# One core, fp32 trunk layer: the gate stage's second half regrouped, its weights' lower parts moved to the vector engine, and the norms' roots taken by a GpSimd power

## The chip, the core and the metric

The kernel runs on one NeuronCore of a Trainium2 chip. The core has a matrix engine (PE), a vector engine (DVE), an activation engine (ACT), GpSimd (POOL) and a sync engine (SP) that issues transfers here. Each works through its own queue in order, and they wait for one another by semaphores. Matmul results land in PSUM banks, from which DVE or ACT fetch them; GpSimd does not touch PSUM in this kernel. The metric is device time in microseconds for one launch. Before the change it is 930.51 us, the median of three runs (929.92 to 930.7).

## The reference

One layer over 1024 tokens and 1024 features, fp32: an input projection feeds a pooling mixer and a gated linear recurrence, an output projection returns to the residual stream `h`, a squared-ReLU MLP follows, and then the part that the change touches most:

```python
def rms_norm(x, g):
    y = x * lax.rsqrt(jnp.mean(x * x, axis=-1, keepdims=True) + RMS_EPS)
    return y * g
...
    z = rms_norm(h, norm_mlp_g[l])
    h = h + jnp.square(jax.nn.relu(z @ w_up[l])) @ w_down[l]
    z = rms_norm(h, norm_ple_g[l])
    gate = jax.nn.sigmoid(z @ w_ple_gate[l] + b_ple_gate[l])
    h = h + gate * (p[l] @ w_ple_proj[l])
return rms_norm(h, norm_final_g)
```

There are four norms: before the input projection, before the MLP, before the gate, and at the end. `w_ple_gate` is 1024x1024, `p` has 256 features.

## The kernel before, in words

Everything is held transposed: features on the 128 partitions, tokens along the free dimension, so `h` is eight tiles `H[0..7]` of 128 features by 1024 tokens. A product of two fp32 matrices is made of three matmuls of a reduced-precision fp32 type: each operand is split into an upper part (an ACT cast, line 176, or 179 with a gain) and a lower part (DVE's difference to it, line 177 or 180), and `mm` (line 340) issues upper·upper, upper·lower and lower·upper, 128 x 128 weights against up to 512 tokens each.

The MLP runs as a fast matrix scheme with seven products per block (`up_pair`, `down`), whose sums DVE builds. The code is a program for a scheduler: it places every instruction on its engine's queue by dependencies and priorities, and `keep_in_program_order` (`pin`), `issue_after` and `high_priority` bind it in places. Buffers come from pools with a fixed number of slots; PSUM offers two double banks (`banks`) and four single ones (`bank`).

A norm (class `Norm`, line 373) squares each tile on ACT, adds the squares on DVE, splits the sum and multiplies it with a matrix of ones on PE, so that each partition holds the sum over all features. `rstd` (line 427) then transposes blocks of 32 on DVE, so that one column in 32 holds all different values, takes square root with scale 1/D and bias eps on ACT (line 436) and the reciprocal on DVE (line 437) of these few columns (`edge`, 16 for 512 tokens, 8 for 256), and transposes them back into `R` (line 438). ACT's functions come in tables; going from one set to another costs a table load on ACT.

The gate stage (lines 1078 to 1136) goes through groups of tokens: 0 to 511, 512 to 767, 768 to 1023. In each group it goes through the eight output tiles in the order `ORDER[g]`. Per output PE does six matmuls for `p @ w_ple_proj` and 24 for the gate (`ple_proj`, `ple_gate`), each as wide as the group. `ple_out` multiplies the gate's bank by `R` on DVE (line 1034), applies the sigmoid on ACT (1035), multiplies with the projection (1040), adds to `h` (1041) and adds the square for the last norm (387, 388). For the last group the operand is normalised beforehand (`ple_in_normed`, 907), so that its sigmoid reads PSUM directly (1032). The weights of outputs 0 to 3 pass through two slots and are fetched again (`FETCH`) for the second and third group, with the lower part on POOL; those of 4 to 7 stay in `B`. When all outputs of a group are done, `finish` (1052) takes the final norm's root and scales each tile of the group by `g_fin` and the root (1058), spread over later outputs by `DONE` and `LAST`, and stores. The last group ends in `finish_last` (1065): gains are applied before the root is known, and four products (1075) and stores follow it.

At the start ten warm-up matmuls on ones run while the first tiles of x arrive (457), and a small activation makes `eps` (371).

Of the kernel before, what the change touches and what calls it, by code (L numbers as in the profile page):

```python
# [12 lines left out]
P = 128  # L13
S = 1024
# [10 lines left out]
AHEAD = ((0,), (1, 2), (3,), ())  # L25
IN = {("P5", 2): (0, 1), ("P5", 3): (2, 3), ("P3", 0): (4, 5), ("P3", 1): (6, 7)}
LATER = ((), (0, 1), (2, 3), (4, 5), (6, 7), (), ())
GROUPS = (slice(0, 512), slice(512, 768), slice(768, 1024))
NT = D // P

ORDER = ((0, 1, 2, 3, 4, 5, 6, 7), (2, 3, 4, 5, 6, 7, 0, 1), (0, 1, 4, 5, 6, 7, 2, 3))

DONE = (((), (), (0,), (1,), (2,), (3,), (4,), (5,)), ((6,), (7,), (), (), (), (), (), ()))
LAST = ((), (), (0, 1), (2, 3), (4, 5), (6, 7), (), ())
FETCH = ((0, 1, 2, 3), (0, 1), (2, 3))
NLRU = 4
NPOOL = 4
WINDOWS = (2, 4, 8, 16)
# [18 lines left out]
def block_kernel(  # L57
# [264 lines left out]
    todo += [(up_step, m, step) for m in range(NPAIR) for step in range(4)]  # L322
    todo += [(down_step, c, kind, q) for c, kind in KINDS for q in range(NQ)]
    for g, os in enumerate(FETCH):
        todo += [
            (load_weights, w_gate[o], f"wg{g}_{o}", S, nc.gpsimd if g else None) for o in os
        ]
    todo.reverse()
    asked = []

# [36 lines left out]
    ones = pool.tile([P, P], F32R, name="ones")  # L367
    nc.vector.tensor_copy(ones, T[4][:, :P])
    ones_f = f32(ones)
    eps = pool.tile([P, 1], F32, name="eps")  # L370
    nc.scalar.activation(eps, ones_f[:, :1], AF.Copy, scale=EPS)

    class Norm:

# [29 lines left out]
        def sums(self, halves=HALVES, cast=False):  # L404

            parts = []
            for hs in halves:
                hi, lo = self.parts(hs)
                o = bank(f"{self.name}_ps{hs.start}")[:, : hs.stop - hs.start]
                in_order[:] = [True] * cast  # L410
                if not cast:
                    nc.vector.tensor_copy(hi, self.acc[:, hs])
                    nc.vector.tensor_tensor(lo, self.acc[:, hs], f32(hi), ALU.subtract)
                pin(nc.tensor.matmul(o, ones, hi, start=True, stop=False))
                pin(nc.tensor.matmul(o, ones, lo, start=False, stop=True))
                in_order.clear()
                parts.append((hs, o))
            return parts

        def sums_of(self, hs, squares):  # L420

            o = bank(f"{self.name}_ps{hs.start}")[:, : hs.stop - hs.start]
            for n, sq in enumerate(squares):
                nc.tensor.matmul(o, ones_f, sq, start=n == 0, stop=n == len(squares) - 1)
            return [(hs, o)]

        def rstd(self, out, parts=None):


            for hs, o in parts or self.sums():  # L430
                r = out[:, hs]
                nc.vector.transpose(r, o)
# [3 lines left out]
                nc.scalar.activation(few, r[:, :, 0], AF.Sqrt, bias=eps, scale=1.0 / D)  # L436
                nc.vector.reciprocal(few, few)
                nc.vector.transpose(r, few.unsqueeze(2).broadcast_to([P, n, 32]))

    def tables():  # L440

        one = ones_f[:, :16]
# [9 lines left out]

    norm = Norm("n0", T[0], T[1:3])
    ps_l = [psum(f"ps_l{o}") for o in range(3)]
    wide = ones.unsqueeze(1).broadcast_to([P, HALF // P, P])
    for _ in range(WARM):
        nc.tensor.matmul(ps_l[2][0][1][:, :HALF], ones, wide, start=True, stop=True)
# [138 lines left out]
    def pool_windows(g, ps):  # L596
        w = WINDOWS[g]
        u, *st = T[:3]
        if ps:
            normed(u, ps)  # L600
        cur = st[g % 2]
        if w == 2:
            nc.vector.tensor_tensor(cur[:, 1:], u[:, 1:], u[:, : S - 1], ALU.add)
            nc.vector.tensor_copy(cur[:, :1], u[:, :1])
        else:

            nc.vector.tensor_tensor_scan(cur[:, :w], ones_f[:, :w], u[:, :w], 0.0, ALU.mult, ALU.add)
# [290 lines left out]
        n = (k % 2) * HALF + hs.start % HALF  # L898
        return [x[:, n : n + hs.stop - hs.start] for x in pair]

    def ple_in(o, hs, norm, to=None):

        to = to or hs
        split(H[o][:, to], *z3(o, to), col("g_ple", o))
# [97 lines left out]
    root = pool.tile([P, 1], F32, name="root")  # L1002

    def ple_psum(g, hs, o, apart):
        turn.append(o)
# [59 lines left out]
    def finish_last(hs, end, squares):  # L1065
# [7 lines left out]
        for o in [*(o for o in range(0, NT, 2) if o != low), low]:  # L1073
            os = slice(o, o + 2)
            nc.vector.tensor_tensor(done[:, os], h_all[:, os, hs], r, ALU.mult)
            nc.sync.dma_start(out_end[:, os], done[:, os])

    for g, hs in enumerate(GROUPS):
        for n, o in enumerate(ORDER[g]):
            pg, pj = ple_psum(g, hs, o, hs == GROUPS[-1] and n == NT - 1)  # L1080
            if g == 0 and n < 2:
                ple_gate(g, hs, o, pg, n == 1)
                held.append((o, pg, pj))
# [7 lines left out]
            elif g == len(GROUPS) - 1 and n == NT - 1:  # L1091
                ple_gate(g, hs, o, pg)
                ple_proj(hs, o, pj)
            else:
                ple_proj(hs, o, pj)
                ple_gate(g, hs, o, pg)
# [3 lines left out]
                split(raw, *B[n + 3])  # L1100
                gate_p[n + 3] = B[n + 3]

            end = g == len(GROUPS) - 1
            if (g > 0 or n > 1) and not (end and n == NT - 1):
                ple_out(hs, o, pg, pj, not end or n < 6)
            if g == 0 and n > 0:
                for o in LATER[n - 1]:
                    ple_in(o, SECOND, norm2, GROUPS[1])
# [4 lines left out]
            if end and n < 6:  # L1113
                gain(o, hs)
            if end and n == NT - 1:
# [11 lines left out]
                in_order.clear()  # L1127
                nc.vector.tensor_tensor(sqs[1], H[o][:, hs], H[o][:, hs], ALU.mult)
                squares += sqs
            if g > 0:  # L1130
                finish(GROUPS[0], DONE[g - 1][n])
# [78 lines left out]
```

## Time and profile before

| | us |
|---|---|
| median of three runs | 930.51 |
| span of the profiled execution, first to last instruction | 929.2 |
| PE busy | 916.9 |
| DVE busy | 766.3 |
| ACT busy | 456.7 |
| POOL busy | 14.9 |

The profiled execution is one of its own; its span does not hold the little that lies before the first and after the last instruction, and 930.51 − 929.2 = 1.3 us stand for that.

In the profile, a group's row names line, engine, operation, output<-inputs (tile names without their numbers), shape and count. A row of the timeline begins with the start and the duration in microseconds; a bracket at its end tells how long the engine was idle before and what released it. "The chain" is the sequence of work that ended last, followed back from the end; its rows are start, duration, engine, tile and line. A row of stretches gives the stretch, its length, and the busy time of PE, weight loads, DVE, ACT and POOL with the number of instructions, then the granted TensorE clock and the transfers' share. Matmuls are pipelined: the duration of one is longer than the distance to the next.

### The profile page before, as it was taken

The numbers are of one execution on the slowest core, as the hardware profiler recorded it, in microseconds if no ns is written. First come the engines' busy times: TensorE is split into PE (matmuls) and PEld (weight loads), VectorE is DVE, ScalarE is ACT, GpSimd is POOL, SyncE is SP. The second block draws the span as 40 slices with busy tenths as digits, with TensorE's granted clock in tenths as the row PEclk, the third lists the DMA queues.
The fourth block names the chain that finished last, engine by engine and source line by source line (L and its number), as shares of the span: only waits on it lengthen the run. The fifth ranks groups of instructions, "written<-read, shape, count | busy, mean of one in ns | idle before, by whom it ended". The sixth has DMA issues, their size and how long they took to land.

```text
span 929.2 us, 11479 instructions
## 1 busy us (share of the span) xinstructions
PE 916.9 (99%) x4472; PEld 804.3 (87%) x4472; DVE 766.3 (82%) x926; ACT 456.7 (49%) x544; POOL 14.9 (2%) x11
## 2 busy tenths in 40 slices
PE   9999999999999999999999999999999999999996
PEld 7888888888888888888888888888888888888995
DVE  7997984669998888888888989979776679885976
ACT  7467892447543443343334545434343446653445
POOL 0000000002000000000000000000000000000220
PEclk9999999999999999999999999999999999999999
DMA  7310143212154355345434998366522441031122
GB/s 259 104 47 25 44 161 111 68 45 75 64 189 161 126 179 194 125 147 187 165 125 157 362 352 272 120 206 209 190 92 91 136 136 45 23 119 41 46 92 91
DMA packets 45189, 125.03 MB, mean 135 GB/s; under 512 B 4176, under 2 KB 6224, under 8 KB 45136
## 3 DMA queue, kind: packets, MB, share of 16 engines
q1 hardware_dynamic: 44992, 124.27, 39.3%
q8 instruction: 35, 0.57, 0.3%
q14 instruction: 18, 0.15, 0.0%
q10 hardware_dynamic: 144, 0.04, 0.0%
HBM read 90.74 MB, written 33.55 MB: 134 GB/s over the span
## 4 chain that ended last, share of the span: by engine, by line
PE 91%; DVE 5%; ACT 2%; DMA 1%; issue 1%; SPq 0%; DVEq 0%; ACTq 0%
PE ps_P_u L350 31%; PE ps_P_d L350 30%; PE ps_i L350 10%; PE ps_o L350 9%; PE ps_e L350 6%; PE ps_l L350 3%; DVE h L1041 1%; PE ps_j L350 1%; DMA wd<-act 1%; PE ps_g L553 1%; DVE a L177 1%; DVE h L1058 1%; DMA h<-in_xT 1%; PE ps_p L350 1%; DVE t L1040 0%
## 5 line engine op out<-in xcount | busy, mean ns | idle before, releaser
L350 PE MATMUL ps_P_d<-a,wd_P_hi 128*128 128x512 f32 x880 | 261.7, 379 | 0.0
L350 PEld LDWEIGHTS ps_P_d<-a,wd_P_hi 128*128 128x128 f32 x880 | 166.3, 189 | 23.6
L350 PE MATMUL ps_P_d<-a,wd_P_lo 128*128 128x512 f32 x440 | 166.9, 379 | 0.7 <-DVE wd_P_lo L177 0.7
L350 PE MATMUL ps_P_u<-a,wu_hi 128*128 128x512 f32 x512 | 152.3, 379 | 0.0
L350 PE MATMUL ps_P_u<-y,wu_hi 128*128 128x512 f32 x384 | 114.0, 379 | 0.0
L350 PEld LDWEIGHTS ps_P_u<-a,wu_hi 128*128 128x128 f32 x512 | 96.8, 189 | 13.8
L350 PE MATMUL ps_P_u<-a,wu_lo 128*128 128x512 f32 x256 | 97.0, 379 | 0.0
L350 PEld LDWEIGHTS ps_P_d<-a,wd_P_lo 128*128 128x128 f32 x440 | 83.2, 189 | 12.9 <-DVE wd_P_lo L177 1.1
L350 PEld LDWEIGHTS ps_P_u<-y,wu_hi 128*128 128x128 f32 x384 | 72.6, 189 | 10.3
L729 DVE TENSOR_TENSOR t<-t,ps_P_u 128x512 f32<-128x512 f32 (+1 forms) x80 | 62.5, 781 | 20.3 <-PE ps_P_u L350 20.2
L350 PE MATMUL ps_i<-a,wi_hi 128*128 128x512 f32 x288 | 74.3, 380 | 0.0
L350 PE MATMUL ps_P_u<-y,wu_lo 128*128 128x512 f32 x192 | 72.8, 380 | 0.0
L177 DVE TENSOR_TENSOR a<-wd,a 128x1024 fp32r<-128x1024 f32 x56 | 67.3, 1218 | 2.4 <-ACT a L176 2.0
L176 ACT ACTIVATE a<-wd 128x1024 fp32r<-128x1024 f32 x56 | 58.8, 1053 | 20.3 <-DMA wd<-act 11.9
L350 PE MATMUL ps_o<-y,wo_hi 128*128 128x512 f32 x256 | 65.7, 379 | 0.0
L350 PEld LDWEIGHTS ps_i<-a,wi_hi 128*128 128x128 f32 x288 | 54.1, 189 | 8.8 <-issue 1.0
L176 ACT ACTIVATE wu_hi<-wu 128x1024 fp32r<-128x1024 f32 x24 | 25.4, 1057 | 69.8 <-PE ps_P_u L350 48.5
L176 ACT ACTIVATE wu_hi<-wu_raw 128x1024 fp32r<-128x1024 f32 (+1 forms) x25 | 25.1, 1006 | 66.9 <-PE ps_P_u L350 41.5
L350 PEld LDWEIGHTS ps_o<-y,wo_hi 128*128 128x128 f32 x256 | 48.4, 189 | 6.8
L350 PEld LDWEIGHTS ps_P_u<-a,wu_lo 128*128 128x128 f32 x256 | 48.4, 189 | 6.8
L176 ACT ACTIVATE wd_P_hi<-wd 128x1024 fp32r<-128x1024 f32 x24 | 25.3, 1054 | 48.9 <-PE ps_P_d L350 44.7
L387 ACT ACTIVATE t<-h 128x512 f32<-128x512 f32 (+2 forms) x47 | 32.8, 697 | 28.0 <-DVE h L1041 19.8
(223 smaller groups left out, 1538.3 us busy)
## 6 DMA issues: line engine op xcount, KB each, us to landing
wd<-act SPq DMA_DIRECT2D x56, 512.0 KB, 5.7
act<-t SPq DMA_DIRECT2D x32, 512.0 KB, 4.4
wu_raw<-in_w_up SPq DMA_DIRECT2D x16, 512.0 KB, 3.5
wu<-in_w_up SPq DMA_DIRECT2D x16, 512.0 KB, 3.9
act<-wu SPq DMA_DIRECT2D x16, 512.0 KB, 4.7
wd<-in_w_down SPq DMA_DIRECT2D x16, 512.0 KB, 6.9
h<-in_xT SPq DMA_DIRECT2D x15, 512.0 KB, 4.2
wg_raw<-in_w_gate SPq DMA_DIRECT2D x12, 512.0 KB, 3.3
```

The costliest lines, as they stand in the source:

```text
L176: first = pin(nc.scalar.activation(hi, src, AF.Copy))
L177: lowest[:] = [pin((eng or nc.vector).tensor_tensor(lo, src, f32(hi), ALU.subtract)).ins]
L350: ins = nc.tensor.matmul(ps, w, turns(z[:, hs]), start=first and z is zhi and w is whi, stop=last and w is wlo, skip_group_check=more,)
L387: nc.scalar.activation(sq, t[:, hs], AF.Square)
L553: nc.tensor.matmul(x, w[r, o * P : (o + 1) * P], turns(z[r, at : at + HALF]), start=n == 0, stop=n == 2)
L729: (eng or nc.vector).tensor_tensor(to, to if y is None else y, x, ALU.add)
L1041: nc.vector.tensor_tensor(hv, hv, e, ALU.add)
L1058: nc.vector.scalar_tensor_tensor(hv, hv, col("g_fin", o), rfin[:, hs], ALU.mult, ALU.mult)
```

## The change

Three things change together.

1. The second 512 tokens are one group of 512 for outputs 2 to 6; only outputs 7, 0 and 1 still run as two groups of 256. So there are four groups, and the weights of outputs 0 and 1 alone are fetched again. The operand is no longer normalised beforehand for the last group: all outputs go through the multiplication by `R` on DVE before the sigmoid. The norm of tokens 512 to 767 is finished during the last two outputs.
2. The lower parts of all gate weights are made on DVE.
3. `rstd` raises the few columns to the power −0.5 with one GpSimd operation, in place of ACT's square root and DVE's reciprocal. The matrix of ones becomes one of 1/D, and eps is folded into the addition of the second square. A first power on 8 columns runs at the start. The `eps` activation and the `root` activation that loaded the square root's table near the end are gone.

```diff
-GROUPS = (slice(0, 512), slice(512, 768), slice(768, 1024))
+GROUPS = (slice(0, 512), slice(512, 1024), slice(512, 768), slice(768, 1024))
-ORDER = ((0, 1, 2, 3, 4, 5, 6, 7), (2, 3, 4, 5, 6, 7, 0, 1), (0, 1, 4, 5, 6, 7, 2, 3))
-DONE = (((), (), (0,), (1,), (2,), (3,), (4,), (5,)), ((6,), (7,), (), (), (), (), (), ()))
-LAST = ((), (), (0, 1), (2, 3), (4, 5), (6, 7), (), ())
-FETCH = ((0, 1, 2, 3), (0, 1), (2, 3))
+ORDER = ((0, 1, 2, 3, 4, 5, 6, 7), (2, 3, 4, 5, 6), (7, 0, 1), (7, 0, 1))
+DONE = ((), (0, 1), (2, 3), (4, 5), (6, 7))
+LAST = ((), (0, 1, 2, 3), (4, 5, 6, 7))
+FETCH = ((0, 1, 2, 3), (), (0, 1), ())
...
-            (load_weights, w_gate[o], f"wg{g}_{o}", S, nc.gpsimd if g else None) for o in os
+        todo += [(load_weights, w_gate[o], f"wg{g}_{o}") for o in os]
...
-    nc.vector.memset(T[4][:, :P], 1.0)
-    nc.scalar.activation(eps, ones_f[:, :1], AF.Copy, scale=EPS)
+    nc.vector.memset(T[4][:, :P], 1.0 / D)
+    nc.vector.memset(power, -0.5)
+    nc.gpsimd.tensor_tensor(spread[:, 64:], one[:, :8], power[:, :8], ALU.pow)
...
-                self.eng.tensor_tensor(self.acc[:, hs], self.acc[:, hs], sq, ALU.add)
+                if n == 1:
+                    self.eng.scalar_tensor_tensor(acc, sq, EPS * D / P, acc, ALU.add, ALU.add)
+                else:
+                    self.eng.tensor_tensor(acc, acc, sq, ALU.add)
...
-                nc.scalar.activation(few, r[:, :, 0], AF.Sqrt, bias=eps, scale=1.0 / D)
-                nc.vector.reciprocal(few, few)
+                nc.gpsimd.tensor_tensor(few, r[:, :, 0], power[:, :n], ALU.pow)
...
-    def ple_in_normed(o, hs):
-        z = T[1 + o % 2][:, hs]
-        nc.vector.scalar_tensor_tensor(z, H[o][:, hs], col("g_ple", o), R[:, hs], ALU.mult, ALU.mult)
-        split(z, *z3(o, hs))
...
-        if hs == GROUPS[-1]:
-            pin(nc.scalar.activation(by(t, pg), got(pg), AF.Sigmoid, bias=col("b_ple", o)))
-        else:
-            nc.vector.tensor_tensor(by(t, pg), got(pg), by(R[:, hs], pg), ALU.mult)
-            nc.scalar.activation(t, t, AF.Sigmoid, bias=col("b_ple", o))
+        nc.vector.tensor_tensor(by(t, pg), got(pg), by(R[:, hs], pg), ALU.mult)
+        pin(nc.scalar.activation(t, t, AF.Sigmoid, bias=col("b_ple", o)))
...
             if g == 1:
-                ple_in_normed(n, GROUPS[2])
+                gain(o, GROUPS[END])
+                finish(FIRST, DONE[n])
...
-                    pin(nc.scalar.activation(root, t[:, :1], AF.Sqrt))
...
-            if end:
-                finish(GROUPS[1], LAST[n])
+            if g == END:
+                finish(GROUPS[END - 1], LAST[n])
```

The scheduler's new order follows from it. On DVE the small operations on the recurrence's parameter move behind the splits of x. At the first norm the second transposition of the first 512 tokens comes ahead of the first one of the second 512. At the second norm both second transpositions come ahead of the lower part of the next MLP weight. On PE the matmuls of the second 512 tokens fall from 480 narrow ones to 150 wide and 180 narrow. ACT's first table load stands in front of the first split of x.

More of the change, by code (lines that the diff above doesn't have):

```diff
@@ L365, in block_kernel @@
     nc.scalar.dma_start(vecs, vec)
-    nc.vector.memset(T[4][:, :P], 1.0)
[L367 to L371, printed above, removed]
+    nc.vector.memset(T[4][:, :P], 1.0 / D)
+    mean = pool.tile([P, P], F32R, name="mean")
+    nc.vector.tensor_copy(mean, T[4][:, :P])
+    mean_f = f32(mean)
+    one = pool.tile([P, 16], F32, name="one")
+    nc.vector.memset(one, 1.0)
+    power = pool.tile([P, 16], F32, name="power")
+    nc.vector.memset(power, -0.5)
+    nc.gpsimd.tensor_tensor(spread[:, 64:], one[:, :8], power[:, :8], ALU.pow)
     class Norm:
@@ L413, in sums @@
                     nc.vector.tensor_tensor(lo, self.acc[:, hs], f32(hi), ALU.subtract)
-                pin(nc.tensor.matmul(o, ones, hi, start=True, stop=False))
-                pin(nc.tensor.matmul(o, ones, lo, start=False, stop=True))
+                pin(nc.tensor.matmul(o, mean, hi, start=True, stop=False))
+                pin(nc.tensor.matmul(o, mean, lo, start=False, stop=True))
                 in_order.clear()
@@ L454, in block_kernel @@
     ps_l = [psum(f"ps_l{o}") for o in range(3)]
-    wide = ones.unsqueeze(1).broadcast_to([P, HALF // P, P])
+    wide = mean.unsqueeze(1).broadcast_to([P, HALF // P, P])
     for _ in range(WARM):
-        nc.tensor.matmul(ps_l[2][0][1][:, :HALF], ones, wide, start=True, stop=True)
+        nc.tensor.matmul(ps_l[2][0][1][:, :HALF], mean, wide, start=True, stop=True)
     for k in range(NT):
@@ L605, in pool_windows @@
         else:
-            nc.vector.tensor_tensor_scan(cur[:, :w], ones_f[:, :w], u[:, :w], 0.0, ALU.mult, ALU.add)
+            nc.vector.tensor_tensor_scan(cur[:, :w], one[:, :w], u[:, :w], 0.0, ALU.mult, ALU.add)
             nc.vector.tensor_tensor_scan(
@@ L1076, in finish_last @@
             nc.sync.dma_start(out_end[:, os], done[:, os])
+    END = len(GROUPS) - 1
     for g, hs in enumerate(GROUPS):
+        last = len(ORDER[g]) - 1
+        if g == END:
+            fin.n[hs.start] = len(ORDER[1])
         for n, o in enumerate(ORDER[g]):
-            pg, pj = ple_psum(g, hs, o, hs == GROUPS[-1] and n == NT - 1)
+            end = g == END and n == last
+            pg, pj = ple_psum(g, hs, o, end)
             if g == 0 and n < 2:
@@ L1090, in block_kernel @@
                     ple_out(hs, o, pg, pj)
-            elif g == len(GROUPS) - 1 and n == NT - 1:
+            elif end:
                 ple_gate(g, hs, o, pg)
@@ L1101, in block_kernel @@
                 gate_p[n + 3] = B[n + 3]
-            end = g == len(GROUPS) - 1
-            if (g > 0 or n > 1) and not (end and n == NT - 1):
-                ple_out(hs, o, pg, pj, not end or n < 6)
+            if (g > 0 or n > 1) and not end:
+                ple_out(hs, o, pg, pj, g < END or n < last - 1)
             if g == 0 and n > 0:
                 for o in LATER[n - 1]:
-                    ple_in(o, SECOND, norm2, GROUPS[1])
+                    ple_in(o, SECOND, norm2)
                 if n == NT - 2:
@@ L1111, in block_kernel @@
             if g == 1:
-                ple_in_normed(n, GROUPS[2])
-            if end and n < 6:
+                gain(o, GROUPS[END])
+                finish(FIRST, DONE[n])
+            if g == END and n < last - 1:
                 gain(o, hs)
-            if end and n == NT - 1:
+            if end:
                 prev = ORDER[g][n - 1]
```

15 lines of the change are left out of this document (5 added, 10 removed).

## The prediction, made before the result was known

> **What bounds the kernel now.** I read the page first (busy shares, then the chain that ended last), then the busy time of each engine in stretches of the last 60 us, then the timeline and the chain around each place that the change touches.
>
> ```profile
> span 929.2 us, 11479 instructions
> PE 916.9 (99%) x4472; PEld 804.3 (87%) x4472; DVE 766.3 (82%) x926; ACT 456.7 (49%) x544; POOL 14.9 (2%) x11
> PE 91%; DVE 5%; ACT 2%; DMA 1%; issue 1%; SPq 0%; DVEq 0%; ACTq 0%
> ...
> 862.40:919.60 57.20, 55.27 (x486) 54.53 (x485) 45.39 (x92) 29.75 (x56) 9.83 (x4) 1.00 0.21 74
> 919.60:929.20 9.60, 1.59 (x6) 0.61 (x5) 4.87 (x10) 2.73 (x6) 0.00 (x0) 0.81 0.29 109
> ```
>
> PE is busy nearly all the time and carries 91% of the chain: what delays a matmul, or what stands after the last one, is the time. The last two rows (its length, then busy us of PE, weight loads, DVE, ACT, POOL) cut the part that the change rewrites: the gate stage's second 512 tokens, from their first matmul to PE's last one before the final norm, take 57.20 us, 1.93 of them idle, and 9.60 us follow in which PE has almost nothing. The stage is called the tail below. The profiled span is 929.2; the median of the three runs is 930.51, so 1.3 us lie around it. I add my differences to 930.51.
>
> **Part 1, one group of 512 for five outputs.** Two rows of the chain give the pace of a matmul, 54 wide ones in the first and 48 of 256 in the second; the next are the steps before the first output store.
>
> ```profile
> 837.50 11.65 PE ps_e L350 x54
> ...
> 913.56 5.36 PE ps_e L350 x48
> ...
> 920.60 0.44 DVE t L1128
> ...
> 921.82 0.46 DVE t L432
> 922.30 0.32 ACT edge L436
> 922.64 0.21 DVE edge L437
> 922.88 0.46 DVE t L438
> 923.36 0.69 DVE t L1075
> ```
>
> A wide matmul is 11.65/54 = 0.2157 us, a narrow one 5.36/48 = 0.1117. One output is 30 of them: 6.47 us wide, twice 3.35 as two halves, so only 0.23 is saved for each output, 1.15 for five. The idle time is the larger part. After the change PE has 150 wide, 180 narrow and about 0.65 us of norm sums: 32.36 + 20.11 + 0.65 = 53.1 us against 57.20, if nothing stalls. So PE ends 4.1 us earlier, at 915.5. I expect no stall, because what made them goes (part 2) and the outputs of 512 leave DVE 6.47 us each for about 3.4 us of its work.
>
> What the chain gives back: the last group's gate is no longer normalised beforehand. Its bank must be multiplied by rstd on DVE before the sigmoid, and the norm of tokens 512 to 767 is now finished during the last two outputs instead of the last six, with eight scalings by g_fin and rstd queued on DVE in between.
>
> ```profile
> 909.11 2.86 DVE L1058 SCALAR_TENSOR_TENSOR h<-h,vecs,t 128x256 f32<-128x256 f32 x7
> ```
>
> From the end of output 0's gate in the last group (911.9 in the new count): multiply and first transpose 0.24 + 0.33 + 0.45, the power (X8, below) with 0.12 of signals, second transpose 0.37, then fourteen operations in DVE's order up to the last square: eight scalings at 2.86/7 = 0.40, six others at 0.34 (0.42 long, started 0.33 apart). That is 1.39 + 0.12 + X8 + 5.24, or 6.8 + X8. PE from the same moment needs 0.22 + 30 narrow matmuls = 3.6. So the last square ends 3.2 + X8 after PE's end; in the rows it ends 1.4 after (921.04 against 919.60): 1.8 + X8 more. The final root: 0.60 us now from the end of the first transpose to the second (922.28 to 922.88), then 0.12 + X8: X8 − 0.48 more. What follows (5.8 us of scaling and stores) stays; the last stores of the group before now leave some 3 us ahead of them, which I count as 0 and at most 0.3.
>
> Tail: −4.1 + 1.8 + X8 − 0.5 + X8 = −2.8 + 2·X8.
>
> **Part 2, lower parts on the vector engine.** Four subtractions on POOL become two on DVE at 1.22 us; two of four refetched weights go, with their 512 KB loads and ACT casts (1.05 each), so SP's queue only gets shorter.
>
> ```profile
> 0.34 0.10 POOL L1197 MEMSET const-uint8-127<- 128x1 uint8 x1
> ...
> 862.99 0.42 DVE L177 TENSOR_TENSOR a<-t,a 128x256 fp32r<-128x256 f32 x1
> 867.75 2.59 POOL L177 TENSOR_TENSOR wg_lo<-wg_raw,wg_hi 128x1024 fp32r<-128x1024 f32 x1 [649.34 <-ACT wg_hi L176]
> 868.44 2.17 DVE L177 TENSOR_TENSOR a<-t,a 128x256 fp32r<-128x256 f32 x1
> ```
>
> A DVE operation of 0.42 us takes 2.17 while POOL works: it ended just behind POOL. Four such holds explain PE's idle time, which part 1 has already counted. The two subtractions fall between outputs of 512, where DVE waits for PE. The splits of 512 columns in place of 256, eight times about 0.3 us, fall before the gate stage under matmuls; the tightest there is the first gate weight's lower part, ready 1.6 us before use. All of that: 0.
>
> **Part 3, roots by a power on GpSimd.** No row shows a power. Linear in columns like the subtraction (2.59 us for 1024, the memset's 0.10 as the fixed part), 16 columns would take 0.14 us; that is the low end. [...] The row nearest to such work is the whole 1024-column subtraction, 2.59: one column of power as much as some sixty of subtraction. The high end is 4 us, half as much again as that. I take X16 = 2.0 and X8 = 1.1, and keep 0.14 and 4.
>
> Where it is hidden: both roots of the first gate groups (a 1.22 us subtraction or 9 us of slack behind them), and the warming call at the start. Where it is not: the tail (counted) and two norms in front of PE.
>
> ```profile
> 35.08 0.72 DVE L432 STREAM_TRANSPOSE rstd<-n_ps 128x512 f32<-128x512 f32 x1 [0.88 <-PE n_ps L415]
> 35.72 1.18 DVE L177 TENSOR_TENSOR wi_lo<-wi_raw,wi_hi 128x1024 fp32r<-128x1024 f32 x1
> 36.83 0.70 DVE L432 STREAM_TRANSPOSE rstd<-n_ps 128x512 f32<-128x512 f32 x1
> 39.40 20.72 PE ps_i L350 x96
> ...
> 252.01 1.31 DVE L432 STREAM_TRANSPOSE rstd<-n_ps 128x512 f32<-128x512 f32 x2
> 253.25 1.18 DVE L177 TENSOR_TENSOR wu_lo<-wu,wu_hi 128x1024 fp32r<-128x1024 f32 x1
> 256.05 2.29 DVE L751 SCALAR_TENSOR_TENSOR t<-t,rstd 128x2048 f32<-128x2048 f32 x1
> 263.85 1.22 DVE L177 TENSOR_TENSOR wu_lo<-wu_raw,wu_hi 128x1024 fp32r<-128x1024 f32 x1
> 264.85 0.59 PE L350 MATMUL ps_P_u<-y,wu_hi 128*128 128x512 f32 x2
> ```
>
> First norm: DVE's new order puts the second transposition of the first half, which waits for POOL, ahead of the first transposition of the second half, which frees a bank that the second matmul of the next projection writes (39.62). POOL reads while DVE's subtraction runs to 36.90; if it must wait for that, as DVE waited above, the bank is free at 38.4 + X16. Stall: X16 − 1.27, so 0.7. Without that wait POOL starts at 35.9 and the stall would be 0; the Trainium skill's page "SBUF — State Buffer", section "Who interferes with whom", says that a DVE instruction with two SBUF inputs and a GpSimd one that reads SBUF share a read interface and that whichever starts first blocks the other, so by that rule the 0.7 stands; this trace shows only the other direction.
>
> Second norm: both transpositions now wait for both powers, and the lower part that filled ACT's 1.28 us table load stands behind them. The 2048-column product moves from 256.05 to 254.6 + 2·X16. DVE runs without a gap from there to the lower part that ends at 265.07, and PE needs it at 265.28. Stall: 2·X16 − 1.65, so 2.35.
>
> The start:
>
> ```profile
> 1.17 1.28 ACT L371 ACT_TABLE_LOAD   x1 [1.17 <-PEq L1197]
> 1.31 4.64 PE L457 MATMUL ps_l<-ones 128*128 128x512 f32 x10 [1.31 <-DVE ones L368]
> 4.14 0.72 ACT L179 ACTIVATE a<-h,vecs 128x512 fp32r<-128x512 f32 x1 [1.48 <-DMA vecs<-in_vec]
> 5.75 1.06 PE L350 MATMUL ps_l<-a,wl_hi 128*128 128x512 f32 x2
> 10.05 1.28 DVE L180 SCALAR_TENSOR_TENSOR a<-h,vecs,a 128x1024 fp32r<-128x1024 f32 x1
> 11.39 0.70 PE L350 MATMUL ps_l<-a,wl_hi 128*128 128x512 f32 x2 [0.37 <-DVE a L180]
> ```
>
> Without the eps activation the table load belongs to the first cast and inherits its wait for x, so the first real matmul moves from 5.75 to about 6.45. But the tiny operations on the recurrence's parameter leave DVE's queue, so the product of 10.05 can start at 9.7 and PE's 0.37 us wait goes: −0.25 at 11.39. Eps folded into one addition for each norm costs 0.06 us there, hidden. The other table loads are off PE's path.
>
> Sum: tail −2.8 + 2.2 = −0.6; norms +0.7 + 2.35; start −0.25: +2.2 us, so 932.7.
>
> **Rivals.** 0.2% of 930.5 is 1.9 us, about what a measurement of this kernel can tell from no change.
> - A short power, X16 up to 0.9: no stall above 0.15 at the norms and a tail of −2.5 to −1.7. At X16 = 0.5 (X8 0.3): −2.2 − 0.25, so 928.1, faster. For it: few columns, and POOL's subtraction is only about twice as slow as DVE's. It decides below 0.9.
> - A middling one, 0.9 to 1.9: 928.7 to 932.4, no change to be told; at 1.45 the two sides cancel (930.5).
> - A long one, above 4 us (lanes one by one): each power then counts about six times, 1 + 2 at the norms and about 1 for both X8 in the tail, and more once POOL outlasts the outputs: 941 at 4.2, about 950 at 6.
> - The clock at the start. The ten warm-up matmuls take 4.64 us, 0.46 each, and the first two real ones (5.75) are as slow, against 0.2157 later: PE starts at half pace. With a gap of 0.7 us behind the warm-up the full pace could come later; 8 more slow matmuls cost about 1.7 us. The Trainium skill's "TensorE: Matmul & The Clock Gate", Part 1, ties the full clock to a busy window of about 3.4 us; by that rule a short gap may or may not spoil one window. One in ten, on top of any case.
>
> **How the numbers follow.** X16 decides, and its row is missing. 1.9 to 4 us gets 0.33 and is the likeliest, with 932.7 (its own range 932 to 941); above 4 gets 0.12; the middle 0.25; the short one 0.30. So slower 0.45, same 0.25, faster 0.30. The range runs from X16 at its low end (−2.8, so 927.7) to 4 us (941).
>
> **What would show it.** Right: a POOL power of 16 columns near 2 us; PE waits behind DVE near 39.5 and 257 to 266; PE's last gate matmul near 915.5 plus those stalls with no idle above 0.3 in the tail; 4 us or more from PE's last output matmul to the last square. Wrong: powers under 0.9 us and no PE wait at the norms (then it is faster); PE idle left in the tail; a later start of the fast pace.

## The result, and the profile after

The changed kernel takes 944.67 us (median of four runs, 942.71 to 945.51) against 930.61 us before (929.92 to 931.19): 1.0149 times as long, 95% interval 1.0137 to 1.016. The forecast was 932.7 us with a range up to 941, so the direction was right and the size was not. The profiled execution has a span of 943.7 us, 14.5 more than the 929.2 before.

The page's busy times and shares of the chain, in the same order as shown of before:

```profile
PE 920.8 (98%) x4322; PEld 800.9 (85%) x4322; DVE 758.7 (80%) x894; ACT 438.8 (46%) x504; POOL 32.8 (3%) x17
PE 85%; DVE 9%; issue 2%; POOL 2%; ACT 1%; DMA 1%; POOLq 0%; DVEq 0%; ACTq 0%
```

PE has 150 matmuls fewer and is still busy longer; its share of the chain fell from 91% to 85%, and DVE's rose from 5% to 9%. The pieces of the chain show where POOL entered it (start, duration, engine, tile, line):

```profile
39.20 3.81 POOL edge L441
44.41 2.91 POOL edge L441
...
261.17 5.80 POOL edge L441 x2
...
926.47 1.65 POOL edge L441
```

These are the powers of the two early norms and that of the final norm for the gate stage's third group (tokens 512 to 767). The groups of POOL's powers say how long one lasts (nanoseconds, least / median / most, then the first and the last start):

```profile
L441 POOL TENSOR_TENSOR edge<-rstd,power x6: 2902/2911/3796, 39.2 to 870.5; 128x16 f32<-128x16 f32 x6
L441 POOL TENSOR_TENSOR edge<-t,power x3: 1635/1635/3646, 890.4 to 935.6; 128x8 f32<-128x8 f32 x2, 128x16 f32<-128x16 f32 x1
L372 POOL TENSOR_TENSOR edge<-one,power x1: 1640/1640/1640, 1.1 to 1.1; 128x8 f32<-128x8 f32 x1
```

16 columns take 2.90 us and 8 take 1.64, so, estimated from these two sizes, a column costs (2.90 − 1.64) / 8 = 0.158 us and the rest 0.38. The prediction took 2.0 and 1.1, between ends of 0.14 and 4.

The longest waits of PE, in total, times and longest:

```profile
PE ps_i L348 <- DVE rstd L437: 4.9, 2, 4.7
PE ps_P_u L348 <- DVE wu_lo L177: 2.8, 1, 2.8
PE n_ps L429 <- ACT t L1118: 2.5, 1, 2.5
```

The first two stand at the first and the second norm, the third behind the last output. To see what each place cost, four moments are enough: the first matmul of the output projection, the first of the MLP's second product, the last gate product of the first 512 tokens, and the end. The first three are the ends of the ranges in the tile's group rows ("first to last start"), the fourth is the span. The rows of after:

```profile
L348 PE MATMUL ps_o<-y,wo_hi x256: 379/379/379, 152.8 to 235.0; 128*128 128x512 f32 x128
L348 PE MATMUL ps_P_d<-a,w x24: 379/379/379, 531.8 to 536.8; 128*128 128x512 f32 x24
L348 PE MATMUL ps_e<-ple,a x96: 379/379/379, 850.7 to 875.5; 128*128 128x512 f32 x96
```

and of before:

```profile
L350 PE MATMUL ps_o<-y,wo_hi x256: 379/379/379, 144.4 to 226.6; 128*128 128x512 f32 x128
L350 PE MATMUL ps_P_d<-a,w x24: 379/379/379, 518.7 to 523.6; 128*128 128x512 f32 x24
L350 PE MATMUL ps_e<-ple,a x96: 379/379/379, 837.3 to 862.2; 128*128 128x512 f32 x96
```

So the stretch up to the output projection, with the first norm in it, is 8.4 us longer (152.8 against 144.4). The next, with the second norm, takes 379.0 against 374.3: 4.7. The next is unchanged (343.7 and 343.5). The tail, from 875.5 to 943.7, takes 68.2 against 67.0: 1.2. Together 14.5. The same four moments were read from every run below:

| kernel | first norm's stretch ends | second norm's stretch | tail | median us |
|---|---|---|---|---|
| before | 144.4 | 374.3 | 67.0 | 930.61 |
| changed | 152.8 | 379.0 | 68.2 | 944.67 |
| power alone | 152.8 | 380.4 | 74.3 | 950.91 |
| changed, all roots back | 146.9 | 374.4 | 65.9 | 932.67 |
| changed, small operations early | 148.9 | 379.1 | 68.2 | 941.05 |
| changed, early roots back | 147.5 | 374.4 | 68.2 | 934.94 |
| changed, PE filled at first norm | 153.0 | 378.8 | 68.2 | 946.27 |
| changed, PE filled at second norm | 151.8 | 379.1 | 68.2 | 944.84 |
| changed, transpositions later | 152.4 | 379.4 | 68.2 | 944.95 |
| power and lower parts, old groups | 151.8 | 378.7 | 67.0 | 944.14 |
| all roots back, small operations early | 143.8 | 374.3 | 66.0 | 930.54 |
| the same, four halves | 143.8 | 374.4 | 64.7 | 928.51 |
| the same, lower parts on POOL | 144.1 | 374.4 | 64.7 | 928.90 |
| lower parts on DVE alone | 144.2 | 374.2 | 64.2 | 928.45 |

One of the four runs of the kernel filled at the first norm took 978.01 us in a slow state and is left out of its median. The kernel before, measured again beside each of these runs, had medians of 930.53 to 930.92 us, and the ratios below are to the one beside. The stretch between the second norm's and the tail, which no edit below touches, takes 342.7 to 344.9 us in these kernels, so the spans of two profiled executions can differ by 2 us for this alone.

### The profile page after: what moved, and what is told of

The parts are those of the page before. It is cut to its first block, busy times and chain, and to the rows that moved or that the text cites. A ratio compares the mean times of both kernels' runs of the same rounds, so it can differ in the third digit from the quotient of the medians.

```text
span 943.7 us, 11100 instructions
## 1 busy us (share of the span) xinstructions
PE 920.8 (98%) x4322; PEld 800.9 (85%) x4322; DVE 758.7 (80%) x894; ACT 438.8 (46%) x504; POOL 32.8 (3%) x17
## 4 chain that ended last, share of the span: by engine, by line
PE 85%; DVE 9%; issue 2%; POOL 2%; ACT 1%; DMA 1%; POOLq 0%; DVEq 0%; ACTq 0%
PE ps_P_u L348 29%; PE ps_P_d L348 29%; PE ps_e L348 10%; PE ps_o L348 9%; PE ps_i L348 3%; PE ps_l L348 3%; DVE h L529 2%; POOL edge L441 2%; PE ps_j L348 1%; DVE wi_lo L177 1%; DMA wd<-act 1%; DVE t L520 1%; DVE y L177 1%; DVE t L611 0%; DVE t L732 0%
```

## The experiments

The theory to test, A in what follows: the power's length in front of the two early norms, and the order of DVE's queue there, make the loss, and the regrouping none of it. Its first rival, B: the regrouping or the lower parts on DVE make a good part of it. C to F are told where they stand.

**Each part by itself.** First part 3 alone: the kernel before with `rstd`, the mean, eps and the start as in the changed kernel.

```diff
-                nc.scalar.activation(few, r[:, :, 0], AF.Sqrt, bias=eps, scale=1.0 / D)
-                nc.vector.reciprocal(few, few)
+                nc.gpsimd.tensor_tensor(few, r[:, :, 0], power[:, :n], ALU.pow)
...
-                    pin(nc.scalar.activation(root, t[:, :1], AF.Sqrt))
```

> The kernel before with part 3 alone (power on POOL, eps and the mean folded in, no table load for eps); groups, order of outputs and lower parts as before. Theory A (the power and what it moves at the two early norms make the whole loss, the regrouping none): the shift of 13.3 us up to the last projection's start stays, and the final root costs 1.64 + 0.12 - 0.60 = 1.2 us more, so about 945 us (943.5 to 946.5). Rival B (the regrouping of the gate stage or the lower parts on DVE carry a good part of it): well below, 931 to 940.

It took 950.91 us, 1.0213 times before (1.0196 to 1.023): 6 us more than the whole change, and above the ranges of both theories. The first norm loses what it loses in the changed kernel, as theory A had it, and the second 1.4 us more (380.4 against 379.0), of which more below. The tail, 74.3 us, is the surprise. PE's longest wait there, and rows of its timeline:

```profile
PE ps_e L350 <- ACT t L1036: 3.9, 1, 3.9
```

```profile
917.31 1.96 DVE L1045 TENSOR_TENSOR h<-h,t 128x256 f32<-128x256 f32 x1
...
922.05 1.85 DVE L1045 TENSOR_TENSOR h<-h,t 128x256 f32<-128x256 f32 x1
```

Two additions of 0.42 us took 1.9 beside POOL's subtractions of weights, with an ACT cast of 1.04 us between them, until a sigmoid freed PE's bank 3.9 us late. The next kernel takes only POOL's subtractions out of this one:

```diff
-            (load_weights, w_gate[o], f"wg{g}_{o}", S, nc.gpsimd if g else None) for o in os
+            (load_weights, w_gate[o], f"wg{g}_{o}") for o in os
```

> The kernel before with the power (950.9 us measured) with the lower parts of its four refetched gate weights on DVE: parts 2 and 3 without the regrouping. Its tail was 74.3 us against 67.0 before and 68.2 in the changed kernel. In its trace PE waited 3.9 us for a sigmoid whose output was late because two DVE operations of 0.4 us took 1.9 behind POOL's subtractions. If those holds make the tail long, 3 to 5 us go: 946 to 948 us. If the narrow groups with their four refetched weights make it long, it stays at 950 to 952.

944.14 us (ratio 1.0146, 1.0131 to 1.0161): the tail went from 74.3 to 67.0, 7.3 us, more than expected. The holds were the cause of the long tail. This kernel lacks only the regrouping and is as fast as the changed one: its tail is 1.2 us shorter. So the same line was tried on the kernel before, with nothing else:

> The kernel before with part 2 alone: the lower parts of the four refetched gate weights on DVE, groups, roots and everything else as before. The 1.93 us of PE idle in the second 512 tokens were put down to POOL's holds. With the power, part 2 by itself was worth 6.8 us (950.9 to 944.1); with roots the tail has only those 1.93 us to give, and the last square follows PE by 1.4 us there: about 1.9 us faster, 928.8 us (928 to 929.6). If the idle has another cause, or the four subtractions of 1.2 us on DVE take the place of the holds, no change: 930.2 to 931.2.

928.45 us, 0.9973 times before (0.9964 to 0.9982): faster, and as forecast. The second 512 tokens run without a gap now (length, busy us of PE, weight loads, DVE, ACT, POOL):

```profile
861.00:917.00 56.00, 56.00 (x493) 55.47 (x492) 43.77 (x100) 30.87 (x58) 0.00 (x0) 1.00 0.22 76
```

Part 2, then, is the part that gains, and it gains alone: 2.8 us of tail. The opposite edit of part 3, the changed kernel with all roots back on ACT and DVE:

```diff
-                nc.gpsimd.tensor_tensor(few, r[:, :, 0], power[:, :n], ALU.pow)
+                nc.scalar.activation(few, r[:, :, 0], AF.Sqrt)
+                nc.vector.reciprocal(few, few)
...
                     pin(nc.scalar.activation(sqs[0], H[prev][:, hs], AF.Square))
+                    pin(nc.scalar.activation(root, t[:, :1], AF.Sqrt))
```

> The changed kernel with the power undone: ACT's square root and DVE's reciprocal give all roots, with the table loaded ahead of the final one as before. Regrouping, lower parts on DVE, folded eps and mean stay. Theory A: no loss at the second norm; at the first the recurrence parameter's 22 small operations still stand in front of the first transposition (3.3 us), which leaves a PE wait of about 1.4 us there and 2 to 3 us in all; the tail gives -0.4 (PE 4.1 earlier, last square later by 1.8 plus a root with its table load of about 1.9). About 932.5 us (931 to 934.5). Rival B: 940 or more.

932.67 us (ratio 1.0023, 1.0013 to 1.0032), as forecast. Twelve of the fourteen microseconds hang on the power. Its tail of 65.9 us stands against 64.2 for part 2 alone: the regrouping costs 1.7 us with roots, as it costs 1.2 with powers. So theory A holds for the early norms, and is wrong in that the regrouping is not free. Then the roots of the two early norms alone:

```diff
+EARLY = ("n0", "n1")
...
-                nc.gpsimd.tensor_tensor(few, r[:, :, 0], power[:, :n], ALU.pow)
+                if self.name in EARLY:
+                    nc.scalar.activation(few, r[:, :, 0], AF.Sqrt)
+                    nc.vector.reciprocal(few, few)
+                else:
+                    nc.gpsimd.tensor_tensor(few, r[:, :, 0], power[:, :n], ALU.pow)
```

> The changed kernel with the roots of the two early norms back on ACT and DVE, the power kept for the norms of the gate stage and the final one. Theory A: as with all roots undone up to the gate stage (first norm 2 to 3 us, second norm 0), then a tail of -2.8 + 2 x 1.64 = +0.5, measured +1.0 in the changed kernel: about 933.5 us (932 to 935.5). The difference to the kernel with all roots undone is what the power is worth in the tail alone: theory A says +1 us, the reverse sign would say that the power does help where ACT changes tables between sigmoid and root. Rival B: 940 or more.

934.94 us (1.0045, 1.003 to 1.006), within its range. Against the run with all roots the power in the tail costs 68.2 − 65.9 = 2.3 us, where 1 was expected.

**The first norm.** In the changed kernel DVE's queue there reads:

```profile
34.52 0.16 DVE L501 TENSOR_SCALAR sp<-sp 128x4 f32<-128x4 f32 x1
...
38.33 0.17 DVE L505 TENSOR_SCALAR sp<-sp 128x4 f32<-128x4 f32 x1
38.41 0.71 DVE L437 STREAM_TRANSPOSE rstd<-n_ps 128x512 f32<-128x512 f32 x1
39.04 1.18 DVE L177 TENSOR_TENSOR wi_lo<-wi_raw,wi_hi 128x1024 fp32r<-128x1024 f32 x1
43.03 0.71 DVE L442 STREAM_TRANSPOSE rstd<-edge 128x512 f32<-128x512 f32 x1 [2.81 <-POOL edge L441]
43.66 0.67 DVE L437 STREAM_TRANSPOSE rstd<-n_ps 128x512 f32<-128x512 f32 x1
44.26 0.65 DVE L520 TENSOR_TENSOR t<-ps_l,rstd 128x512 f32<-128x512 f32 x1
47.35 0.71 DVE L442 STREAM_TRANSPOSE rstd<-edge 128x512 f32<-128x512 f32 x1 [2.44 <-POOL edge L441]
47.99 1.18 DVE L177 TENSOR_TENSOR hl<-t,hl 128x1024 fp32r<-128x1024 f32 x1
49.09 1.21 DVE L520 TENSOR_TENSOR h<-ps_l,rstd 128x1024 f32<-128x1024 f32 x1
```

Twenty operations on the recurrence's parameter (`sp`, 0.2 us apart) fill DVE from 34.52 until the first transposition at 38.41, which before started at 35.08: 3.33 us. Then DVE idles 2.81 and 2.44 us behind the powers. Line 520 in the last row starts 8.45 us later than before (40.64, line 517 there). To part the two causes, the small operations were given priority:

```diff
-    nc.vector.tensor_scalar_mul(neg, lv, -1.0)
...
+    with tc.high_priority():
+        nc.vector.tensor_scalar_mul(neg, lv, -1.0)
...
```

> The changed kernel with the recurrence parameter's small operations given priority, so that they leave DVE's queue during the first projection, and nothing else changed. Theory A: the first norm's transposition is back at 35.1 us; with a power of 2.9 us plus 0.8 behind DVE's subtraction the PE wait of 4.7 shrinks to about 1.4 and little slow clock follows: 3.5 to 5 us less than the changed kernel, about 940.5 us (939.5 to 941.5). Rival C (the power alone decides at the first norm, the small operations only fill DVE's wait for it): less than 1 us changes, 943.7 to 945.

941.05 us (1.0115, 1.01 to 1.013), as theory A had it. PE's wait there is 1.5 us, and yet the stretch still ends 4.5 us late. With this edit and that of all roots together, DVE's same operation can be compared directly.

> All roots on ACT and DVE again, and the recurrence parameter's small operations with priority: both causes at the first norm taken away, regrouping and lower parts on DVE kept. If the two explain the first norm, its remaining 2.5 us go: 932.7 - 2.5 = 930.2 us (929.4 to 931.2). If the 2.5 us came from something else in the change (the eps addition, the missing early table load), it stays near 932.5.

930.54 us (0.9997, 0.9987 to 1.0006): the two causes explain the first norm wholly. Line 521 (520 in the changed kernel) with the power, and line 522, the same operation, with roots:

```profile
45.22 1.21 DVE L521 TENSOR_TENSOR h<-ps_l,rstd 128x1024 f32<-128x1024 f32 x1
```

```profile
39.97 1.21 DVE L522 TENSOR_TENSOR h<-ps_l,rstd 128x1024 f32<-128x1024 f32 x1
```

45.22 − 39.97 = 5.25. DVE's idle time behind POOL in this run is again 2.81 + 2.44 = 5.25; that the two agree to the hundredth is partly chance, for smaller differences between the two queues (a later first transposition, no reciprocals) nearly cancel. The stretch is 5.1 us longer (148.9 against 143.8). PE's wait is 1.5.

That DVE's row carries the rest of the stretch with it is seen in every trace. In thirteen of the fourteen kernels the output projection starts 103.6 to 103.8 us after this row, whatever PE did in between: 103.7 in the changed kernel (152.8 − 49.09), where PE waits 4.7 us and its matmuls are slow behind the wait, 103.7 with the small operations early (148.9 − 45.22), where it waits 1.5 and they are not, and 103.8 with the roots back as well (143.8 − 39.97), where it does not wait.

**What bounds the stretches behind the norms.** Behind both waits PE's matmuls ran at half pace for a while, 0.43 us apart in place of 0.2157. The stretches of the changed kernel, with the granted clock as the third number from the right:

```profile
45.00:60.00 15.00, 15.00 (x65) 12.93 (x64) 12.65 (x12) 4.28 (x4) 2.32 (x1) 0.91 0.11 36
265.00:275.00 10.00, 7.18 (x26) 5.66 (x25) 7.71 (x9) 2.63 (x3) 1.96 (x1) 0.83 0.33 121
```

Whether the slow matmuls cost time was tested by keeping PE busy where it waits, with matmuls into the bank that is next overwritten. The first kernel, with 22 matmuls at the first norm; the second has `0, 13` in the first line:

```diff
+FILL1, FILL2 = 22, 0
...
         ps = psum(f"ps_i{i}")
+        for _ in range(FILL1 if i == 0 else 0):
+            nc.tensor.matmul(ps[0][1][:, :HALF], mean, wide, start=True, stop=True)
...
             ps = mlp_bank(f"ps_{kind}_u{m}")
+            for _ in range(FILL2 if (m, kind) == (1, "P7") else 0):
+                nc.tensor.matmul(ps, mean, wide, start=True, stop=True)
```

> The changed kernel with 22 more matmuls (4.7 us at full pace, their result is overwritten) ahead of the next projection's first one, where PE waits 4.7 us at the first norm, so that PE is busy there and the clock has no reason to drop. Theory D (DVE's chain of transpositions and convolutions sets the end of the stretch from 39 to 117 us, PE's wait and its slow matmuls are inside it): no change from the changed kernel, 944 to 945.5. Theory E (the slow matmuls behind the wait cost their 1.5 us): about 943 us.

> The changed kernel with 13 more matmuls (2.8 us, overwritten) ahead of the product that waits 2.8 us at the second norm. Theory E there: the wait's own length stays, but the 12 matmuls at 0.43 us behind it return to 0.2157, and 1.8 us are gained: about 942.9 us (942.3 to 943.6). Rival: the slow pace has another cause (the same clock drop with PE busy, or DVE as the bound behind it), no change: 944 to 945.5.

946.27 us (1.017, 1.0149 to 1.019) and 944.84 us (1.0157, 1.0142 to 1.0172): no gain in either. The clock did recover. The same stretches, the first norm's with 22 matmuls added there, then the second norm's with 13 added there, and a row of the latter's timeline:

```profile
45.00:60.00 15.00, 15.00 (x72) 13.12 (x71) 13.88 (x13) 4.49 (x4) 1.08 (x1) 1.00 0.11 36
```

```profile
265.00:275.00 10.00, 10.00 (x47) 8.45 (x46) 8.63 (x10) 3.24 (x4) 0.98 (x1) 1.00 0.43 156
```

```profile
277.38 0.48 PE L349 MATMUL ps_P_u<-y,wu_lo 128*128 128x512 f32 x1 [1.45 <-DVE wu_lo L178]
```

At the second norm there are 47 matmuls in ten microseconds, 13 of them the added ones, in place of 26, and no gain: PE waits for DVE again at 277, and the stretch takes 379.1 us against 379.0. Theory E is out there.

The filling at the first norm is not so clean a test. In its trace DVE's first transposition comes at 37.17, 1.24 us earlier than in the changed kernel (where the small operations are late, it lies anywhere from 37.2 to 38.4), and then the scheduler's order of DVE's and ACT's work is another one between 60 and 80 us, in which DVE loses that again: this is the one kernel whose output projection starts 105.1 us behind DVE's row. So it cannot tell whether 1.5 us were gained at the wait. That theory E is out at the first norm rests on the comparison above: the stretch ends as far behind DVE's row with slow matmuls as without. Why the order is another one stays open; the 0.8 us by which the span exceeds the changed kernel's lie in the MLP's second product (344.5 against 343.7).

The slow matmuls are slack that DVE leaves, but only so much of it. The kernel with the power alone and the same with its lower parts on DVE are alike up to the gate stage. At the second norm PE waits 2.8 us in both, behind which the clock was 0.66 in the first and 1.00 in the second (rows in the last section), and the stretch took 380.4 and 378.7 us. In the first, DVE later waited for PE:

```profile
276.95 0.69 DVE L734 TENSOR_TENSOR t<-t,ps_P_u 128x512 f32<-128x512 f32 x1 [0.67 <-PE ps_P_u L350]
```

So 1.7 us hang on the slow pace in that execution, and some 0.3 at 0.83, as in the changed kernel (379.0).

The last run of this kind moves only the product's wait. The lower part that PE waits for goes ahead of the transpositions that wait for POOL:

```diff
-            norm.rstd(R, norm.sums(cast=True))
+            norm.rstd(R, norm.sums(cast=True), later)
...
             with tc.issue_after(up_lower[1, 2]):
+                for r, full in later:
+                    nc.vector.transpose(r, full)
```

> The changed kernel with the two second transpositions of the second norm, which wait for POOL, issued on DVE behind the lower part that PE waits 2.8 us for, and nothing else moved. Theory D (DVE's idle time behind POOL is the loss, 2.43 + 2.17 us there): that lower part now fills 1.2 us of it, but the power beside it may take 0.8 longer: 943.5 to 944.6 us, and PE waits somewhere behind instead. Theory F (PE's wait for that lower part and the slow matmuls behind it are the loss): 2.8 + 1.8 us go, about 940 us.

944.95 us (1.0147, 1.013 to 1.0164): a little above theory D's range and far from theory F. A PE wait of 2.9 us is still there, behind a later lower part and with slow matmuls behind it (granted clock 0.83 from 275 to 285), and DVE still idles behind POOL. The wait, and DVE's rows:

```profile
PE ps_P_u L348 <- DVE wu_lo L177: 2.9, 1, 2.9
```

```profile
263.74 0.71 DVE L862 STREAM_TRANSPOSE rstd<-edge 128x512 f32<-128x512 f32 x1 [1.33 <-POOL edge L441]
266.62 0.71 DVE L862 STREAM_TRANSPOSE rstd<-edge 128x512 f32<-128x512 f32 x1 [2.17 <-POOL edge L441]
```

The lower part filled 1.10 us of DVE's idle time (2.43 to 1.33), and the product behind the transpositions started 115.0 us into the stretch in place of 115.9, yet the stretch is no shorter (379.4 against 379.0). So theory F is out: the wait for that one lower part is not the loss. But theory D is not shown by this run either, for an earlier DVE gained nothing while PE's wait moved on. What is shown at the second norm is that the 4.7 us are gone with the early roots back (374.4), and that filling PE's wait gains nothing.

**The regrouping, mended.** With roots and early small operations, the last square still stood behind scalings of the finished group. Four outputs in place of five as one group leave one more narrow output to hide them:

```diff
-ORDER = ((0, 1, 2, 3, 4, 5, 6, 7), (2, 3, 4, 5, 6), (7, 0, 1), (7, 0, 1))
-DONE = ((), (0, 1), (2, 3), (4, 5), (6, 7))
-LAST = ((), (0, 1, 2, 3), (4, 5, 6, 7))
+ORDER = ((0, 1, 2, 3, 4, 5, 6, 7), (2, 3, 4, 5), (6, 7, 0, 1), (6, 7, 0, 1))
+DONE = ((), (0, 1), (2, 3, 4), (5, 6, 7))
+LAST = ((), (0, 1, 2, 3), (4, 5, 6, 7), ())
```

The kernel just before, in the expectation, is the one with all roots back and the small operations early.

> The kernel of the run just before with four outputs of the second 512 tokens as one group in place of five, so that four narrow outputs stand behind the norm of tokens 512 to 767 and its eight scalings on DVE are done before the last output's sigmoid. PE's end moves by 0.23 us later; the last square, now held 2.2 us by scalings, follows it more closely: about 2 us less, 928.3 us (927.3 to 929.5). If the last square is held by something else, 930 or more.

928.51 us (0.998, 0.9971 to 0.9989), faster than both kernels of the case, as forecast. Its tail of 64.7 us is still not below the 64.2 of the lower parts on DVE alone. The last, with POOL making its two lower parts again:

```diff
-            (load_weights, w_gate[o], f"wg{g}_{o}") for o in os
+            (load_weights, w_gate[o], f"wg{g}_{o}", S, nc.gpsimd if g else None) for o in os
```

> The kernel with four halves (all roots on ACT and DVE, small operations early) with the lower parts of the two refetched gate weights back on POOL: part 2 undone by itself. The prediction's price for part 2 is the end of the POOL holds: there are two subtractions of about 2.6 us, each holds a DVE operation for up to 1.8 us. In the stretch of 512-wide outputs DVE has about 3 us of slack for each output, so theory A says 0 to +1.5: 928.5 to 930 us. If the holds reach PE as they did before the change (1.93 us of idle there from four of them), 930 or more.

928.90 us (0.998, 0.9971 to 0.9989), with the same tail of 64.7. POOL's two subtractions fall into the stretch of wide outputs (870.32 and 876.79) and cost nothing that can be told; four among narrow ones cost 2.8 us.

## Why the prediction was wrong

- *The power's length* (2.0 and 1.1 taken) was 2.90 and 1.64, inside its ends. No row of before held a power, and of what work it consists no run shows; the two numbers were a choice between bounds far apart. By the prediction's own terms that gives 1.63 at the first norm, 4.15 at the second, +0.5 in the tail and −0.25 at the start: 6.0 us, 936.5. So the mis-sized length explains 3.8 of the missing 12 us. Of the rest, about 7 lie at the first norm.
- *First norm, "Stall: X16 − 1.27"* is the step that failed, and the largest miss: 8.4 us were lost in its stretch. It priced PE's wait, and PE's wait is not what bounds there; and it left out the small operations (next point). With these out of the way the wait was 1.5 us, about what the formula says at 2.90 (1.63), but DVE idled 5.25 us and the stretch was 5.1 us longer than with roots. The profile of before showed the bound:

```profile
45.00:60.00 15.00, 15.00 (x71) 12.89 (x69) 15.00 (x14) 5.43 (x5) 0.00 (x0) 1.00 0.09 32
60.00:80.00 20.00, 20.00 (x103) 16.73 (x103) 18.84 (x22) 14.68 (x16) 0.00 (x0) 1.00 0.23 79
80.00:100.00 20.00, 20.00 (x99) 17.00 (x98) 14.53 (x17) 19.42 (x21) 0.00 (x0) 1.00 0.09 26
```

  PE is busy throughout, and so is DVE (15.00 of 15.00, then 18.84 of 20). From 80 to 100 us DVE has gaps, but there ACT is nearly full (19.42 of 20), and DVE waits for it, 4.3 us at the longest, before and in the changed kernel alike. In such a stretch the time that DVE idles at its start is not made up, as the constant 103.7 us shows.
- *"the tiny operations on the recurrence's parameter leave DVE's queue"* was right about where they left and silent about where they went: ahead of the first transposition. That is worth 3.9 us in the stretch with the power (152.8 against 148.9) and 3.1 with roots (146.9 against 143.8). That they move behind the splits of x was known before the result.
- *That POOL would wait behind DVE's subtraction* held: the power beside it took 3.80 us instead of 2.90, and 1.02 us of the two overlapped. By the Trainium skill's "SBUF — State Buffer", section "Who interferes with whom", the two share a read interface and the order of issue decides who blocks; the traces agree where DVE comes first. Where the power came first they do not (last section).
- *Second norm, "Stall: 2·X16 − 1.65"* gives 4.15 at 2.90, and 4.7 were lost. The 2048-column product did move as forecast: it starts 115.9 us into the stretch in place of 111.7, 4.3 later (254.6 + 2·2.90 − 256.05 = 4.35). PE's wait came at an earlier lower part than the one named; with that one moved ahead it came at a later one.
- *Start, −0.25*: the steps came as described. The first real matmul starts at 6.34 (about 6.45 forecast), the product at 9.50 (9.7), and the wait at 11.39 is gone. The gain cannot be told: PE's first norm sum starts at 34.09 in place of 34.41, but at 33.71 to 34.50 in the other kernels, with 34.15 in the one whose start is that of before.
- *Tail, −2.8 + 2·X8*: +0.5 at 1.64, and 1.2 measured. PE's part, 875.74 to 928.93, took 53.2 us without any idle (53.1 forecast), and the last square ended 4.8 us after PE's outputs (3.2 + 1.64 = 4.84). The missing 0.7 lies behind the last square, and most of it is PE itself: after a wait of 2.5 us its sums ran at half pace, 1.22 us in place of the 0.70 of before, and of the 0.60 ahead of the wait. A row of before and two of after:

```profile
921.08 0.70 PE L424 MATMUL n_ps<-t,ones 128*128 128x256 f32 x2 [0.58 <-DVE t L1128]
```

```profile
928.93 0.60 PE L429 MATMUL n_ps<-t,mean 128*128 128x256 f32 x2
933.78 1.22 PE L429 MATMUL n_ps<-t,mean 128*128 128x256 f32 x2 [0.51 <-DVE t L1124]
```

- *Part 1, −4.1, and part 2, "All of that: 0"*: the sum was near, the shares were not. The idle time was part 2's alone, and so was the gain (−2.8). The narrow groups' last square followed PE by 1.4 us; with the regrouping and the power it follows by 4.8, which takes back more than the matmuls save.
- The rival *"A long one, above 4 us"* is out by the power's length, and *"The clock at the start"* by the start. That the clock would drop at the norms was in no rival; it did, and cost little in the changed kernel (some 0.3 us at the second norm, none to be seen at the first).

## What to carry to other kernels

A wait is priced on the engine that has no slack behind it, not on the one that has the longest wait in the list. Read the busy times of the stretch that follows: where two engines are both full, idle time of either counts, and here keeping the other busy gained nothing. Edits that share a diff are worth pricing one by one: here one line of the three parts gains 0.27% by itself, and the two others hide it. And a scheduler that moves small operations off one place puts them somewhere else; look where.

## What the runs showed of the hardware

The granted clock answers the same wait differently. With the same 2.8 us wait of PE at the second norm, the rows of the kernel with the power alone and of the same kernel with its lower parts on DVE, which are alike up to there, are:

```profile
265.00:275.00 10.00, 7.17 (x20) 5.47 (x19) 7.70 (x9) 2.64 (x3) 2.00 (x1) 0.66 0.33 119
```

```profile
265.00:275.00 10.00, 7.18 (x34) 6.29 (x34) 8.70 (x10) 3.20 (x4) 0.95 (x1) 1.00 0.43 160
```

0.66 and 1.00, and 0.83 in the changed kernel, with 20, 34 and 26 matmuls in much the same busy time. Waits of 1.2 to 1.5 us left the clock at 1.00 in their stretches. The Trainium skill's "TensorE: Matmul & The Clock Gate", Part 1, has the half-rate clock follow an idle window of about 3.4 us, and the windows run freely. A wait of 2.8 us is shorter than such a window, and the clock fell behind it in two of these three kernels; here the measurement decides. The windows themselves no run shows.

A power was held by a DVE subtraction that already ran, and did not hold one that started later. The three longer powers of the changed kernel (3.80, 3.73 and 3.65 us for 16 columns) began 0.16, 0.22 and 0.31 us into a subtraction of 1.18 us, so the less of it was left, the less was lost. In the run with later transpositions a subtraction began 0.44 us into a power:

```profile
260.79 5.80 POOL L441 TENSOR_TENSOR edge<-rstd,power 128x16 f32<-128x16 f32 x2 [34.37 <-DVE rstd L437]
261.23 1.18 DVE L177 TENSOR_TENSOR wu_lo<-wu,wu_hi 128x1024 fp32r<-128x1024 f32 x1
```

It took 1.18 us, as it does with no power beside it, and the two powers 2.90 each. This is the one such overlap in these traces.

The power's first execution, at the start, took 1.64 us like the later ones of its size; no cost of a first call is seen in its row.
